# A retention layer's v made in its own head, with the next head's k and q projections between the head's steps

## The chip, the core and the metric

The kernel runs on one core of a Trainium2 chip. The metric is the device time of one launch in microseconds (us). The kernel before takes 1476.63 us, the median of three runs (1476.28 to 1478.8). The engines are named as the profile names them: PE is TensorE (matmuls; PEld are its weight loads), DVE is VectorE, ACT is ScalarE, POOL is GpSimd, SP is SyncE, which issues most of the DMAs.

## The reference

One inference step of a decoder with two layers, on 512 prompt tokens and 8 groups of 4 sample tokens together (544 columns). Layer 0 mixes with a short gated convolution, layer 1 with multi-scale retention; each is followed by a gated feed-forward part. The change lies in the retention layer (4 heads, keys of 256, values of 512, model width 1024):

```python
def retention_mixer(x, s0, pos, w_in, gn_g, w_out):
    q, k, v, g = jnp.split(x @ w_in, [1024, 2048, 4096], axis=-1)   # then by heads
    q, k = rotary(q, pos), rotary(k, pos) * 256 ** -0.5
    o, S = retention_chunkwise(q, k, v, s0)   # o = (q k^T * decay) v + q S0 * decay
    o = (o - mean(o)) * rsqrt(var(o) + 1e-6)                         # over a head's 512 values
    return (silu(g) * o * gn_g) @ w_out, S    # S: the new state, prompt and every sample row
```

## The kernel before

Activations stand with the model width on the partitions: 8 tiles of 128 x 544. Every f32 product is made of three rounded ones (hi x hi, hi x lo, lo x hi): `split` makes the rounded part on ACT (L188) and the rest on DVE (L189); `load_piece` brings a weight piece of 512 KB by SP and splits it, with three buffers for each of the raw piece, its high and its low part (tags `w`, `wh`, `wl`). `project` multiplies a piece with the activations: 8 k-tiles x 3 products x 2 halves of 272 columns, 48 matmuls on L175. PSUM has two double banks (`psum()`, printed as `mm`) and four single banks (`bank()`, printed as `sm`).

The order of the work is written by hand, and a planner that knows costs fixes the sequence on each engine: an instruction that is ready may go ahead of an earlier one that is not. `tc.issue_after(ins)` holds a block's instructions behind `ins` on their engine.

The stages are: convolution layer, feed-forward part 0, `ahead`, the four heads of retention, feed-forward part 1.

- `ahead` (L847 to 917) runs at the end of feed-forward part 0. It makes k and q of head 0, and completes R (L259), the broadcast of the token norms. In between stands `value_products(0, ...)`, which makes v of head 0 and sends it to DRAM (`v_made`). With R, `operand` makes on DVE and ACT the four operand tiles of the gate jobs, one for each pair of k-tiles, each of seven planes: planes 0 to 4 by a first split, 5 and 6 by a second. The tile that it works in has the tag `f` with two buffers. Then come six gate jobs (L461): gates of heads 0 to 2, each job a fast matrix product of seven products of 12 matmuls instead of eight (`Job`, `weights7`). Results go to DRAM (`gate_made`).
- A head `h` (L1299 to 1391) that has a next one starts with `value_products(h + 1, ...)`: 96 matmuls of 512 columns in four pieces (L816 to L818) and the sample tokens' share (L824). Through `first` and `then` this head's own v is loaded and split (`value_loaded`), the states are loaded (`states_load`), the head's q and k are split and transposed (`operands_made`), and the sample v is gathered (`value_sample`). `value_out` sends the next head's v to DRAM by ACT's queue. Then come `state` (the prompt's state, in two halves), `first_outputs` (the samples against their first state S0, its update, and the load of the fourth, S3, into its buffer), `scores`, `inner` 0 to 3, `normalized` (on DVE, with the root on POOL), `gated` (a transpose on PE, then a product with the gates on DVE), `states_update` (outer products, then two passes on DVE, L1258).
- Four `qk_project` for the next head stand among the later steps: k's two halves around the last states, with `states_update(h, st, 3)` inside the second, and q's two halves after the last `gated_pair`, right before `out_project`. A projection's end scales its half (`qk_rotate`, L1002), and after the second half `rotate` turns it (L1011 to 1016).
- `out_project` (L1261) splits the gated values (yh on ACT, yl on DVE) and multiplies them with four pieces of the output weights.
- Head 3 has no next head; its gates are made by four `gate_project` in the places of the others' projections.

Of the kernel before, what the change touches and what calls it, by code (L numbers as in the profile page):

```python
# [12 lines left out]
P = 128  # L13
# [35 lines left out]
def hybrid_decode_kernel(ctx: ExitStack, tc: tile.TileContext, a: dict, o: dict):  # L49
# [741 lines left out]
    v_made = [dram.tile([P, 5, DV], F32, tag=f"v{h}", name=nm("vm")) for h in range(NH)]  # L791
    gate_made = [dram.tile([P, 4, T], F32, tag=f"g{h}", name=nm("gm")) for h in range(AHEAD)]

    def value_piece(h, c, raw, adding=False, after=None, sw=None):
        return load_piece(a["rtv"][h, c], 2 * DV, keep=raw, adding=adding, after=after, sw=sw)

    def value_products(h, xs, first=None, then=None, ws=None, sw=None):

        pv = [bank() for _ in range(4)]
        pvs = psum()  # L800
        if ws is None:
            raw = []
            ws = [value_piece(h, c, raw, first is None, sw=None if c else sw) for c in range(2)]
        else:
            ws, raw = ws
        after = first() if first is not None else None
        for c in range(4):
            wh, wl = ws[c]
            if c < 2:
                ws.append(value_piece(h, c + 2, raw, first is None and c == 0, after=after if c == 0 else None))  # L810
            for k2 in range(2):
                kt = 2 * c + k2
                cw = slice(k2 * DV, (k2 + 1) * DV)
                for tt in range(4):
                    ts_, out = slice(tt * P, (tt + 1) * P), pv[tt]
                    nc.tensor.matmul(out, xh[kt][:, ts_], wh[:, cw], start=(kt == 0), stop=False)  # L816
                    nc.tensor.matmul(out, xh[kt][:, ts_], wl[:, cw], start=False, stop=False)  # L817
                    last = nc.tensor.matmul(out, xl[kt][:, ts_], wh[:, cw], start=False, stop=(kt == KT - 1))  # L818
            if c in (1, 2):

                with tc.issue_after(last.ins):
                    for g in range(4):
                        kt = 4 * (c - 1) + g
                        nc.tensor.matmul(  # L824
                            pvs[g * NS : (g + 1) * NS, 0, :], xs[:, kt, :],
                            raw[kt // 2][:, kt % 2 * DV : (kt % 2 + 1) * DV],
                            start=(c == 1), stop=(c == 2), skip_group_check=True,
                        )
            if then is not None:
                then(c)  # L830
        return pv, pvs

    def value_out(h, pv, pvs, places):

        for tt, (row, _) in enumerate(places):
            nc.scalar.activation(
                row, pv[tt] if tt < 4 else pvs[:, 0, :], AF.Copy, scale=rN[:, tt : tt + 1] if tt < 4 else rN[:, 5:6]
            )
            if places[tt][1] is not None:
                at, src = places[tt][1]  # L840
                nc.scalar.dma_start(v_made[h][:, at, :], src)
# [5 lines left out]
    def ahead(tp, fp, sw, one):  # L847
# [10 lines left out]
        qw, qpt = load_piece(a["rtqk"][0, 0], KT * P, adding=True), [bank(), bank()]  # L858
        project(qpt, *qw, 0, xh, xl, weave=steps)
# [11 lines left out]
        off(0, 0, qpt)  # L871
        xs = fp.tile([P, KT, NS], F32, tag="f", name=nm("xs"))
        sample_x(xs)

        def operand_of(c):
# [3 lines left out]
        va = [tp.tile([P, 2, T], F32, tag="gu", name=nm("va")) for _ in range(2)]  # L879
        vs = fp.tile([P, DV], F32, tag="f", name=nm("vs"))  # L880
        rows = [va[tt // 2][:, tt % 2, :DV] for tt in range(4)] + [vs]
        outs = [None, (slice(0, 2), va[0][:, :, :DV]), None, (slice(2, 4), va[1][:, :, :DV]), (4, vs)]
        qw = load_piece(a["rtqk"][0, 1], KT * P, adding=True)
# [38 lines left out]
    with ExitStack() as c2:  # L922
# [39 lines left out]
        def qk_start(h):  # L962

            st = {}
            gt = tp.tile([P, 2, T], F32, tag="gt", name=nm("gt"), bufs=1)
            nc.sync.dma_start(gt, a["gtab"][h])
            st["gt"] = gt
            st["rot"] = [
                tp.tile([P, 2, T], F32, tag=f"rot{w}", name=nm("rot"), bufs=1) for w in range(2)
            ]  # L970
            return st

        def qk_loaded(st):

            loads = [(st["rot"][1], qk_made[1]), (cos, a["rope"][0]), (sin, a["rope"][1]), (st["rot"][0], qk_made[0])]
            for t, src in loads:
                last = nc.sync.dma_start(t, src)
# [9 lines left out]
        def qk_project(h, st, which, dt, inside=None):  # L987

            wh, wl = load_piece(a["rtqk"][h, which * 2 + dt], KT * P)
            pt = [bank(), bank()] if dt else psum()  # L990
# [8 lines left out]
        def qk_rotate(st, which, dt, pt):  # L999
            r = st["rot"][which]  # L1000
# [24 lines left out]
        def value_loaded(h, st):  # L1025

            vw = tp.tile([P, 4, T], F32, tag="gate", name=nm("vw"), bufs=1)[:, :, :DV]
            vsw = tp.tile([P, DV], F32, tag="yn", name=nm("vsw"))
            nc.sync.dma_start(vw, v_made[h][:, 0:4, :])
            st["loaded"] = nc.sync.dma_start(vsw, v_made[h][:, 4, :])  # L1030
            vh = tp.tile([P, 4, DV], F32R, tag="vyh", name=nm("vh"), bufs=1)
            vl = tp.tile([P, 4, DV], F32R, tag="vyl", name=nm("vl"), bufs=1)
            for i in range(2):
                split(vh[:, 2 * i : 2 * i + 2, :], vl[:, 2 * i : 2 * i + 2, :], vw[:, 2 * i : 2 * i + 2, :])
            st["v"] = [vh, vl, vsw]
            if h < AHEAD:
                st["gate"] = tp.tile([P, 4, T], F32, tag="gate", name=nm("gate"), bufs=1)
                nc.sync.dma_start(st["gate"], gate_made[h])

        def value_sample(h, st):  # L1040

            pt = psum()
            v4 = tp.tile([P, 2, DV], F32R, tag="rot1", name=nm("v4"), bufs=1)
            split(v4[:, 0, :], v4[:, 1, :], st["v"][2])
            for i in range(2):
                nc.tensor.matmul(pt[:NS, 0, :], sum4, v4[:, i, :], start=(i == 0), stop=(i == 1))
            v2 = [tp.tile([NS, DV], F32R, tag=f"rt{i}", name=nm("v2"), bufs=1) for i in range(2)]
            split(*v2, pt[:NS, 0, :])
            st["v"][2] = v2
# [249 lines left out]
        for h in range(NH):  # L1299
            more = h + 1 < NH  # L1300
            st["S"] = {}

            def first():
                value_loaded(h, st)
                return st["loaded"] if h == 0 else None

            def then(c):
                if c == 0:
                    with tc.issue_after(last_load[0].ins) if h == 0 else ExitStack():
                        for i in range(2):  # L1310
                            states_load(h, st, i)
                elif c == 1:
                    states_load(h, st, 2)
                    operands_made(h, st)
                elif c == 2:
                    value_sample(h, st)

            if more:
                pv, pvs = value_products(h + 1, xs, first, then, None if h else next_v)
                va = tp.tile([P, 2, DV], F32, tag="rot1", name=nm("va"), bufs=1)  # L1320
                vb = [tp.tile([P, DV], F32, tag="yn", name=nm("vb")) for _ in range(2)]
                sample_operands(h, st)
                vc = tp.tile([P, DV], F32, tag="rt1", name=nm("vc"), bufs=1)
                rows = [va[:, 0, :], va[:, 1, :], *vb, vc]
                outs = [None, (slice(0, 2), va), (2, vb[0]), (3, vb[1]), (4, vc)]
                value_out(h + 1, pv, pvs, list(zip(rows, outs)))
                state(h, st, 0)
                first_outputs(h, st)
                state(h, st, 1)
            else:  # L1330
                gw = load_piece(a["rtg"][h, 0], KT * P)
                first()
# [181 lines left out]
```

## Time and profile before

| what | before |
| --- | --- |
| median of three runs | 1476.63 us |
| the profiled execution's own time | 1478.13 us |
| its span, first to last instruction | 1475.8 us |
| PE busy | 1458.5 us (99%) |
| DVE busy | 959.6 us (65%) |
| ACT busy | 610.5 us (41%) |
| POOL busy | 90.1 us (6%) |
| mean granted PE clock | 0.995 |
| DMA | 194.86 MB, mean 132 GB/s |

A busy time is the union of an engine's instructions in the one profiled execution; matmuls overlap in it, so the time from the start of one to the start of the next says more than the duration of one. The granted clock is the share of full speed at which PE was allowed to run. In the groups of instructions a row has: line, engine, operation, out<-in by tile names, shapes, count | busy us, mean ns of one | idle us of the engine just before them, and what ended it.

### The profile page before, as it was taken

Reading aid. Unit: us, or ns where it says so; the run is one execution under the profiler, and the core shown is the slowest. Engines: PE = TensorE matmul, PEld = TensorE weight load, DVE = VectorE, ACT = ScalarE, POOL = GpSimd, SP = SyncE. Lnnn points to the kernel's source line nnn. Section 1 sums busy time; section 2 is a strip of 40 time slices with the busy share of each in tenths; the row PEclk is TensorE's granted clock in tenths of the full one; section 3 lists DMA queues with packets and bytes.
Section 4 is the critical chain, followed back from the end, with each engine's and each line's share of the span. In section 5 each row is a group of like instructions: output and inputs, shape, how many; then the busy total and the mean of one; then the engine's idle time right before and its main releaser. Section 6 shows DMA issues by size and latency. Waiting matters only on the chain.

```text
span 1475.8 us, 26100 instructions
## 1 busy us (share of the span) xinstructions
PE 1458.5 (99%) x10944; PEld 1382.9 (94%) x10944; DVE 959.6 (65%) x1470; ACT 610.5 (41%) x882; POOL 90.1 (6%) x112
## 2 busy tenths in 40 slices
PE   9999999999999999999899999999999999999998
PEld 9999999999999999799589698798799999999997
DVE  6645439847748546776686484595759857748645
ACT  5222355625425335466412322323265625525424
POOL 0100220000000003000000000000030000000002
PEclk9999999999999999999999999999999999999999
DMA  6222274232222334554784573672454232322322
GB/s 225 86 87 86 89 177 109 96 105 87 93 93 100 98 90 132 140 169 149 274 287 140 197 257 115 210 248 102 157 146 112 94 107 86 99 93 96 101 65 83
DMA packets 77445, 194.86 MB, mean 132 GB/s; under 512 B 7168, under 2 KB 24448, under 8 KB 76944
## 3 DMA queue, kind: packets, MB, share of 16 engines
q1 hardware_dynamic: 70272, 172.83, 34.6%
q0 software_dynamic: 2912, 10.56, 4.1%
q10 hardware_dynamic: 4144, 9.81, 1.7%
q8 instruction: 86, 1.41, 0.4%
q14 instruction: 31, 0.25, 0.1%
HBM read 162.29 MB, written 30.88 MB: 131 GB/s over the span
## 4 chain that ended last, share of the span: by engine, by line
PE 94%; DVE 3%; DMA 1%; issue 1%; ACT 1%; POOL 0%; DVEq 0%; POOLq 0%; ACTq 0%; SPq 0%
PE mm L175 35%; PE sm L461 30%; PE sm L175 15%; PE sm L817 2%; PE sm L818 2%; PE sm L163 2%; PE sm L816 2%; PE sm L1237 1%; PE sm L164 1%; PE sm L165 1%; DVE wl L189 1%; DMA wl<-in_rtqk_dram 1%; PE mm L1253 0%; DVE xl L201 0%; PE mm L1192 0%
## 5 line engine op out<-in xcount | busy, mean ns | idle before, releaser
L188 ACT ACTIVATE wh<-w 128x1024 fp32r<-128x1024 f32 (+4 forms) x210 | 204.5, 977 | 382.8 <-PE mm L175 185.7
L189 DVE TENSOR_TENSOR wl<-w,wh 128x1024 fp32r<-128x1024 f32 (+4 forms) x210 | 236.9, 1131 | 42.5 <-ACT wh L188 40.4
L461 PE MATMUL sm<-oh,wh 128*128 128x272 f32 x672 | 194.5, 289 | 0.0
L461 PE MATMUL sm<-oh,wl 128*128 128x272 f32 x672 | 194.2, 289 | 0.0
L461 PE MATMUL sm<-ol,wh 128*128 128x272 f32 x672 | 194.0, 289 | 0.0
L175 PE MATMUL mm<-xh,wh 128*128 128x272 f32 x804 | 170.1, 292 | 0.2
L175 PE MATMUL mm<-xh,wl 128*128 128x272 f32 x804 | 167.0, 290 | 2.4 <-DMA wl<-in_rtqk_dram 2.4
L175 PE MATMUL mm<-xl,wh 128*128 128x272 f32 x804 | 166.8, 289 | 0.0
L269 DVE TENSOR_TENSOR x<-x,mm 128x544 f32<-128x544 f32 x85 | 61.3, 721 | 144.3 <-PE mm L175 144.1
L461 PE MATMUL sm<-oh,l 128*128 128x272 f32 x504 | 145.6, 289 | 0.0
L461 PE MATMUL sm<-ol,h 128*128 128x272 f32 x504 | 145.4, 289 | 0.0
L461 PE MATMUL sm<-oh,h 128*128 128x272 f32 x504 | 145.3, 289 | 0.0
L175 PEld LDWEIGHTS mm<-xh,wl 128*128 128x128 f32 x804 | 126.1, 190 | 3.2 <-DMA wl<-in_rtqk_dram 2.6
L175 PEld LDWEIGHTS mm<-xh,wh 128*128 128x128 f32 x804 | 126.7, 190 | 1.7 <-ACT wh L188 0.5
L461 PEld LDWEIGHTS sm<-oh,wh 128*128 128x128 f32 x672 | 126.8, 189 | 1.1 <-ACT u L518 0.6
L175 PEld LDWEIGHTS mm<-xl,wh 128*128 128x128 f32 x804 | 127.0, 190 | 0.1
L461 PEld LDWEIGHTS sm<-oh,wl 128*128 128x128 f32 x672 | 126.8, 189 | 0.0
L461 PEld LDWEIGHTS sm<-ol,wh 128*128 128x128 f32 x672 | 126.6, 188 | 0.0
L189 DVE TENSOR_TENSOR l<-w,h 128x1024 fp32r<-128x1024 f32 x84 | 80.3, 956 | 56.3 <-ACT h L188 56.0
L175 PE MATMUL sm<-xh,wh 128*128 128x272 f32 x476 | 101.6, 291 | 0.0
L175 PE MATMUL sm<-xh,wl 128*128 128x272 f32 x476 | 99.8, 288 | 0.0
L175 PE MATMUL sm<-xl,wh 128*128 128x272 f32 x476 | 99.5, 287 | 0.0
(290 smaller groups left out, 3049.4 us busy)
## 6 DMA issues: line engine op xcount, KB each, us to landing
w<-in_ffgu_dram SPq DMA_DIRECT2D x88, 512.0 KB, 3.5
w<-in_ffdn_dram SPq DMA_DIRECT2D x96, 192.0 KB, 2.5
S<-in_rets_dram SPq DMA_DIRECT2D x16, 1024.0 KB, 7.1
out_rets_dram<-S SPq DMA_DIRECT2D x16, 1024.0 KB, 4.6
w<-in_cvin_dram SPq DMA_DIRECT2D x21, 512.0 KB, 3.4
w<-in_rtv_dram SPq DMA_DIRECT2D x16, 512.0 KB, 3.7
w<-in_rtqk_dram SPq DMA_DIRECT2D x16, 512.0 KB, 4.3
w<-in_rtg_dram SPq DMA_DIRECT2D x16, 512.0 KB, 3.8
```

The lines of the kernel that those rows point to most:

```text
L163: nc.tensor.matmul(out, lh, rh, start=start, stop=False, skip_group_check=True)
L164: nc.tensor.matmul(out, lh, rl, start=False, stop=False, skip_group_check=True)
L165: last_product[0] = nc.tensor.matmul(out, ll, rh, start=False, stop=stop, skip_group_check=True)
L175: last_product[0] = nc.tensor.matmul(half(pt, hf)[:, :HT], w[:, c], act[k][:, hf * HT : (hf + 1) * HT], start=(first and k == ks[0] and i ...
L188: h = nc.scalar.activation(dh, src, AF.Copy)
L189: nc.vector.tensor_sub(dl, src, dh.bitcast(F32))
L269: last_residual[0] = nc.vector.tensor_add(xk, xk, p)
L461: nc.tensor.matmul(out, w[:, c], b[k][:, at, :], start=(first and k == 0 and i == 0), stop=(k == n - 1 and i == 2), skip_group_check=True,)
L816: nc.tensor.matmul(out, xh[kt][:, ts_], wh[:, cw], start=(kt == 0), stop=False)
L817: nc.tensor.matmul(out, xh[kt][:, ts_], wl[:, cw], start=False, stop=False)
L818: last = nc.tensor.matmul(out, xl[kt][:, ts_], wh[:, cw], start=False, stop=(kt == KT - 1))
L1237: last_product[0] = nc.tensor.matmul(st["po"][32 * g : 32 * g + 8, :], qm[:, dt, g, r, :], st["S"][i][:, g, :], start=False, stop=(i == 3) ...
```

## The change

v is made at the beginning of its own head, from PSUM straight into the two parts that the products read; nothing of v goes to DRAM. The four projections of the next head's k and q are spread: k's first half behind the values, k's second around `inner` 0, q's first around a `gated_pair` and `inner` 3, q's second around `states_update` 3 and the last `gated_pair`. In `ahead` head 0's q and k are made without v, copied by ACT without R (the scaling with R comes when they are read back), and the operands of the gate jobs are made while q's second half is projected. Head 3 makes its own v first, and its `first_outputs` stand behind the scores.

```diff
     def ahead(tp, fp, sw, one):
...
-        qw, qpt = load_piece(a["rtqk"][0, 0], KT * P, adding=True), [bank(), bank()]
-        project(qpt, *qw, 0, xh, xl, weave=steps)
+        qs = [load_piece(a["rtqk"][0, dt], KT * P, adding=True) for dt in range(2)]
+        qpts = [[bank(), bank()], psum()]
+        project(qpts[0], *qs[0], 0, xh, xl, weave=steps)
         drain(steps)
...
-            each(lambda p, d, r: nc.vector.tensor_mul(d, p, r), pt, halves(made[which][:, dt, :]), R)
+            each(lambda p, d: nc.scalar.activation(d, p, AF.Copy), pt, halves(made[which][:, dt, :]))
...
-        pv, pvs = value_products(0, xs, then=operand_of, sw=sw)
-        ...
-        value_out(0, pv, pvs, list(zip(rows, outs)))
-        qpt = psum()
-        project(qpt, *qw, 0, xh, xl)
-        off(0, 1, qpt)
+        for c in range(KP):
+            operand(c, fp, oh, ol, lambda kt: g_mix(1, kt))
+        project(qpts[1], *qs[1], 0, xh, xl)
+        off(0, 1, qpts[1])
...
-                next_v.extend(([value_piece(1, c, raw) for c in range(2)], raw))
+                next_v.extend(([value_piece(0, c, raw) for c in range(2)], raw))
...
             for which in (1, 0):
                 r = st["rot"][which]
+                qk_scale(st, which)
                 nc.vector.tensor_mul(r, r, st["gt"][:, which, :].unsqueeze(1).to_broadcast([P, 2, T]))
                 rotate(st, which)
...
+        def value(h, st, ws=None):
+            pv = [bank() for _ in range(4)]
+            pvs = psum()
+            ws, raw = ws or ([], [])
+            for c in range(4):
+                if len(ws) == c:
+                    ws.append(value_piece(h, c, raw))
+                ...          # 24 matmuls of a piece; after pieces 1 and 3 the sample tokens' share
+                if c == 1:
+                    operands_made(h, st)
+            ...              # sample v: v4 from pvs by ACT and DVE, gathered by sum4, split
+            for tt in range(4):
+                nc.scalar.activation(vh[:, tt, :], pv[tt], AF.Copy, scale=rN[:, tt : tt + 1])
+                nc.vector.scalar_tensor_tensor(
+                    vl[:, tt, :], pv[tt], rN[:, tt : tt + 1], vh[:, tt, :].bitcast(F32),
+                    op0=ALU.mult, op1=ALU.subtract,
+                )
+            st["v"] = (vh, vl, v2)
...
         for h in range(NH):
             more = h + 1 < NH
+            value(h, st, None if h else next_v)
             st["S"] = {}
+            for i in range(3):
+                states_load(h, st, i)
             if more:
+                st["gate"] = tp.tile([P, 4, T], F32, tag="gate", name=nm("gate"), bufs=1)
+                nc.sync.dma_start(st["gate"], gate_made[h])
+                nxt = qk_start(h + 1)
+                for which in (1, 0):
+                    qk_scale(nxt, which)
+                qk_project(h + 1, nxt, 1, 0)
+            else:
+                gate_project(h, st, 0)
+            sample_operands(h, st)
+            state(h, st, 0)
+            if more:
+                first_outputs(h, st)
+            else:
+                gate_project(h, st, 1)
+            state(h, st, 1)
+            for c in range(2):
+                scores(h, st, c)
+            if more:
+                yn = {}
+                def first():
+                    yn[0] = normalized(inner(h, st, 0))
+                    sample_outputs(h, st, 1)
+                    states_update(h, st, 1)
+                def second():
+                    gated_pair(h, st, (yn[0], 0), (yn[1], 1))
+                    yn[3] = inner(h, st, 3)
+                def third():
+                    states_update(h, st, 3)
+                    gated_pair(h, st, (yn[4], 4), (yn[3], 3))
+                qk_project(h + 1, nxt, 1, 1, first)
+                yn[1] = normalized(inner(h, st, 1))
+                sample_outputs(h, st, 2)
+                p2 = inner(h, st, 2)
+                qk_project(h + 1, nxt, 0, 0, second)
+                yn[2] = normalized(p2, "rt1")
+                with tc.issue_after(last_product[0].ins):
+                    sample_outputs(h, st, 3)
+                states_update(h, st, 2)
+                yn[3] = normalized(yn[3])
+                yn[4] = normalized(st["po"])
+                gated(h, st, yn[2], 2)
+                qk_project(h + 1, nxt, 0, 1, third)
                 out_project(h, st)
             else:
+                first_outputs(h, st)
+                ...          # inner 0 to 2 and the updates between them, as before
```

`qk_project` with a function as its last argument multiplies four k-tiles, calls the function, and multiplies the other four, into two single banks. The tile of the rotated q (`rot0`) is now taken when its first half is written, since `mid` of the head has the same buffer until `inner` 3.

More of the change, by code (lines that the diff above doesn't have):

```diff
@@ L790, in hybrid_decode_kernel @@
     qk_made = [dram.tile([P, 2, T], F32, tag=f"qk{w}", name=nm("qkm")) for w in range(2)]
-    v_made = [dram.tile([P, 5, DV], F32, tag=f"v{h}", name=nm("vm")) for h in range(NH)]
     gate_made = [dram.tile([P, 4, T], F32, tag=f"g{h}", name=nm("gm")) for h in range(AHEAD)]
[L794 to L841, printed above, removed]
+    def value_piece(h, c, raw):
+        return load_piece(a["rtv"][h, c], 2 * DV, keep=raw)
     def sample_x(xs):
@@ L967, in qk_start, with rotated @@
             st["gt"] = gt
[L968 to L971 removed]
+            st["rot"] = [None, rotated(1)]
+            return st
+        def rotated(which):
+            return tp.tile([P, 2, T], F32, tag=f"rot{which}", name=nm("rot"), bufs=1)
         def qk_loaded(st):
+            st["rot"][0] = rotated(0)
             loads = [(st["rot"][1], qk_made[1]), (cos, a["rope"][0]), (sin, a["rope"][1]), (st["rot"][0], qk_made[0])]
             for t, src in loads:
[L977 removed]
+                nc.sync.dma_start(t, src)
             for which in (1, 0):
                 r = st["rot"][which]
+                qk_scale(st, which)
                 nc.vector.tensor_mul(r, r, st["gt"][:, which, :].unsqueeze(1).to_broadcast([P, 2, T]))
@@ L989, in qk_project @@
             wh, wl = load_piece(a["rtqk"][h, which * 2 + dt], KT * P)
-            pt = [bank(), bank()] if dt else psum()
+            pt = [bank(), bank()] if inside else psum()
             if inside:
@@ L999, in qk_rotate @@
         def qk_rotate(st, which, dt, pt):
+            if which == 0 and dt == 0:
+                st["rot"][0] = rotated(0)
             r = st["rot"][which]
@@ L1040, in value_sample @@
[L1040 to L1049, printed above, removed]
+            for tt in range(4):
+                nc.scalar.activation(vh[:, tt, :], pv[tt], AF.Copy, scale=rN[:, tt : tt + 1])
+                nc.vector.scalar_tensor_tensor(
+                    vl[:, tt, :], pv[tt], rN[:, tt : tt + 1], vh[:, tt, :].bitcast(F32),
+                    op0=ALU.mult, op1=ALU.subtract,
+                )
@@ L1318, in hybrid_decode_kernel @@
-            if more:
[L1319 to L1332, printed above, removed]
-                for i in range(2):
-                    states_load(h, st, i)
-                gate_project(h, st, 0, lambda: operands_made(h, st), gw)
-                value_sample(h, st)
-                states_load(h, st, 2)
-                sample_operands(h, st)
-                state(h, st, 0)
-                first_outputs(h, st)
-                gate_project(h, st, 1)
-                state(h, st, 1)
@@ L1343, in hybrid_decode_kernel @@
-            for c in range(2):
-                scores(h, st, c)
-            yn0 = normalized(inner(h, st, 0))
-            sample_outputs(h, st, 1)
-            yn1 = normalized(inner(h, st, 1))
-            states_update(h, st, 1)
-            sample_outputs(h, st, 2)
-            p2 = inner(h, st, 2)
-            if more:
+            for i in range(3):
+                states_load(h, st, i)
+            if more:
+                st["gate"] = tp.tile([P, 4, T], F32, tag="gate", name=nm("gate"), bufs=1)
+                nc.sync.dma_start(st["gate"], gate_made[h])
```

78 lines of the change are left out of this document (30 added, 48 removed).

## The prediction

> **What bounds the kernel now.** I read the page's span and its chain first, then the waits of TensorE (PE) alone, then the window table around each wait, then the timelines of the three places that the diff rearranges.
>
> ```profile
> span 1475.8 us, 26100 instructions
> ...
> PE 94%; DVE 3%; DMA 1%; issue 1%; ACT 1%; POOL 0%; DVEq 0%; POOLq 0%; ACTq 0%; SPq 0%
> ```
>
> The chain that ends last is PE for 94%. The diff leaves the number and the shapes of the matmuls as they are: the value products of four heads, the 16 projections for q and k, the gates and the small sample products all stay, in another order. So the time can move only through the moments in which PE waits or runs at a lower clock. Before the change these are few (waits of PE: us in total, times, longest):
>
> ```profile
> PE mm L175 <- DMA wl<-in_rtqk_dram: 2.4, 1, 2.4
> PE sm L816 <- ACT wh L188: 2.3, 1, 2.3
> PE sm L817 <- DVE wl L189: 2.0, 1, 2.0
> ...
> PE sm L1192 <- DVE yn L1168: 0.6, 1, 0.6
> ```
>
> The first three lie in parts that the diff rewrites: one in `ahead`, before the gate jobs, two at the start of head 0. Heads 1 to 3 have no longer wait than the 0.6 of the last row, so a gain can come only from these places, and everything else can only be kept or lost. They also cost clock (the window table: busy us of PE, PEld, DVE, ACT and POOL, then the granted PE clock, DMA share and GB/s):
>
> ```profile
> 624.77:628.19 3.42, 3.42 (x18) 3.42 (x17) 1.05 (x2) 2.71 (x4) 0.00 (x0) 0.50 0.79 240
> 713.51:716.94 3.43, 3.43 (x8) 2.76 (x9) 3.43 (x8) 1.28 (x2) 0.00 (x0) 0.50 0.83 320
> ```
>
> Soon after the first wait, and after the last of the two at head 0, PE works for 3.4 us at half the clock, which loses 1.7 us each time.
>
> **Part 1: `ahead` without v.** Before, PE has q's first half, then head 0's value products, then q's second half, while R (the broadcast of the norm) is completed and VectorE (DVE) makes from it the operands of the gate jobs. The change takes the value products out of that place.
>
> ```profile
> 591.28 0.40 ACT L259 ACTIVATE R<-sm 128x272 f32<-128x272 f32 x1 [0.28 <-PE sm L227]
> 595.66 0.39 PE L816 MATMUL sm<-h,xh 128*128 128x512 f32 x1
> ```
>
> ```profile
> L189 DVE TENSOR_TENSOR ol<-f,oh 128x1360 fp32r<-128x1360 f32 (+1 forms) x8 | 9.2, 1150 | 6.1 <-ACT oh L188 6.1
> L534 DVE SCALAR_TENSOR_TENSOR f<-x,vec,R 128x544 f32<-128x544 f32 x8 | 6.0, 780 | 0.1
> L189 DVE TENSOR_TENSOR wl<-w,wh 128x1024 fp32r<-128x1024 f32 x2 | 2.4, 1218 | 0.0
> L404 DVE TENSOR_TENSOR f<-f 128x272 f32<-128x272 f32 x4 | 1.8, 441 | 0.1
> ...
> L403 DVE TENSOR_TENSOR f<-f 128x272 f32<-128x272 f32 x4 | 1.7, 435 | 0.0
> ```
>
> R is complete at 591.28 + 0.40 = 591.7. The four operands then cost DVE 9.2 + 6.0 + 7.0 = 22.2 us (the last are the four sums L403, L404, L406 and L407 of 1.7 to 1.8, of which the first and the last row are shown). The first product needs all four, but only their first split (planes 0 to 4), so the last operand's L406, L407 and second split, some 1.6 us, come after it: 20.6 us are left, and one of the weight splits of the first job (1.2 us) lies among them. With no bubble the last first split is done at 591.7 + 21.8 = 613.5. ACT's turn in the middle of each operand, which is the 6.1 us of idle time in the first row, hides now: `xs` no longer holds one of the two buffers of tag `f`, and the copies of k and q move from DVE to ACT. The rest of job 0's weight work fits before R, when DVE is idle:
>
> ```profile
> 580.00:592.00 12.00, 12.00 (x100) 12.00 (x100) 0.54 (x3) 5.05 (x7) 3.98 (x4) 1.00 0.58 117
> ```
>
> PE leaves q's first half at 595.66 and has one projection left. From the chain, a projection and a row of gate-job products:
>
> ```profile
> 630.83 60.68 PE sm L461 x480
> ```
>
> ```profile
> 748.60 5.97 PE mm L175 x48
> ```
>
> The projection ends at 601.6. A gate-job matmul takes 60.68/480 = 0.126 us. While the last operand is missing, products 1, 5 and 2 can run on three of their four k: 3 x 3 x 3 = 27 matmuls, 3.4 us. PE then idles 613.5 - 601.6 - 3.4 = 8.5 us if the planner interleaves them so, 11.9 if not, and perhaps 6 if weight splits stay out of DVE's way and products of the next job slip in. I take 8.5, and half of one half-clock stretch (0.9), since part of it would fall into the idle time. Gone are the 2.4 us wait and its 1.7. Sum: 8.5 + 0.9 - 4.1 = **+5.3** (ends +2 and +9.5).
>
> **Part 2: the start of head 0.** The place of the same instruction in three heads gives the cost of that start:
>
> ```profile
> 705.13 0.40 PE L817 MATMUL sm<-wl,xh 128*128 128x512 f32 x1
> 705.37 0.40 PE L818 MATMUL sm<-wh,xl 128*128 128x512 f32 x1
> 705.69 1.06 PE L824 MATMUL mm<-w,xs 128*32 128x512 f32 x8
> ```
>
> ```profile
> 815.23 1.07 PE L824 MATMUL mm<-w,xs 128*32 128x512 f32 x8
> ```
>
> ```profile
> 917.37 1.06 PE L824 MATMUL mm<-w,xs 128*32 128x512 f32 x8
> ```
>
> From head 0 to head 1 there are 109.5 us, from 1 to 2 102.1: head 0 loses 7.4. It waits because v comes back from memory:
>
> ```profile
> 705.06 2.01 ACT L188 ACTIVATE vh<-vw 128x1024 fp32r<-128x1024 f32 x2 [7.84 <-DMA vw<-vm]
> ```
>
> ```profile
> 706.15 1.22 DVE L189 TENSOR_TENSOR vl<-vw,vh 128x1024 fp32r<-128x1024 f32 x1 [2.26 <-ACT vh L188]
> ...
> 710.47 0.72 DVE L1016 TENSOR_TENSOR rot<-rot,rt 128x544 f32<-128x544 f32 x1
> ```
>
> ACT stands 7.8 us at this load with the weight split of piece 2 queued behind it, and DVE stands 2.3 us behind ACT with q's rotation queued behind v's split. After the change there is no such load. Pieces 0 and 1 are there as before; piece 2 has a free buffer and nothing that blocks SP in front of it. On DVE one split of 1.2 and a wait of 2.3 go, two scalings of `gt` (0.7 each, like any 128x544 product) and piece 2's split (1.2) come: q's rotation ends near 711.2 - 3.5 + 2.6 = 710.3. PE has piece 2's 24 matmuls, 0.24 apart, until 705.69 + 1.06 + 5.7 = 712.4, so it need not wait for the rotation. Piece 3 may come up to 2 us late, because its buffer is free only after L824. I take **-6.5** (ends -7.4 and -5).
>
> New on DVE are four evictions of v from PSUM; the nearest row is another PSUM read of this size:
>
> ```profile
> L1168 DVE TENSOR_SCALAR yn<-sm,mv,rs 128x512 f32<-128x512 f32 x5 | 4.0, 804 | 0.0
> ```
>
> Four of 0.8 come for two of 1.2 that go, under the k projection (6 us) that follows: 0, and 0.8 a head without that cover.
>
> **Part 3: the end of heads 0 to 2.** Here the change gives cover away.
>
> ```profile
> 874.97 0.60 PE L1192 MATMUL mm<-cb,yn 128*128 128x128 f32 x4
> ...
> 882.02 0.41 PE L175 MATMUL mm<-yh,wh 128*128 128x272 f32 x2
> 882.27 0.41 PE L175 MATMUL mm<-yl,wh 128*128 128x272 f32 x2
> ```
>
> ```profile
> 879.29 0.72 DVE L189 TENSOR_TENSOR yl<-gate,yh 128x544 fp32r<-128x544 f32 x1
> ```
>
> The last gated transposes end at 875.57 and `out_project` starts at 882.02: 6.45 us of projections cover the chain of gated product, yh on ACT, yl on DVE. The first yl is done at 880.01 and read at 882.27, so 2.3 us are spare. In the new order the last pair stands in the middle of q's second projection, with 3.0 us of cover: 1.2 us are uncovered by that alone. `states_update(h, st, 3)`, which stood inside k's second projection, now stands right before the pair:
>
> ```profile
> L1258 DVE SCALAR_TENSOR_TENSOR S<-S,mm 128x1024 f32<-128x1024 f32 x8 | 9.6, 1208 | 3.1 <-PE mm L1253 3.1
> ```
>
> Its two passes are ahead of the gated products on DVE: up to 2.4 more. q's own scaling and the rest of its rotation compete with yl as well. On the other side PE can begin the first k of three outputs before it needs the second yl (some 2 us). I take **3.0 a head, +9.0** for three (ends 0 and 6 a head). DVE is busy enough for this: 39 of 52 us in the stretch that ends there.
>
> ```profile
> 829.20:881.40 52.20, 52.20 (x348) 42.02 (x347) 39.18 (x64) 14.36 (x21) 3.56 (x5) 1.00 0.75 256
> ```
>
> **Part 4: the rest.** In the last head `first_outputs` moves behind the scores, so the fourth state, S3, gets its buffer later. Its update takes 2.4 us, and then comes the trip out and in:
>
> ```profile
> S<-in_rets_dram SPq DMA_DIRECT2D x16, 1024.0 KB, 7.1
> out_rets_dram<-S SPq DMA_DIRECT2D x16, 1024.0 KB, 4.6
> ```
>
> Together 14 us, against 18 inner products of 0.24 and one and a half gate projections of 6.0, 13 us, and some small products: +0.7 (0 to 3). In the other heads the loads of S0 to S2 now queue on SP behind the pieces of v, but v's own products and the k projection, over 20 us, stand before their use: 0, and up to one landing of 7.1 if that cover were gone. v's writes on ACT's queue and its loads on SP's are gone.
>
> Sum: 5.3 - 6.5 + 9.0 + 0.7 = **+8.5**. The profiled execution took 1478.13 (span 1475.8 and 2.3 around it), 1.5 above the median of 1476.63; so 1486.6 for its like, 1485.1 as a median.
>
> [...] The first wait above was 2.4 us, and the clock then fell to 0.50 for 3.42 us. [...]
>
> **Rivals.** *Cover holds at the tails* (11%, faster). It decides whether the first yl lands before q's last matmul; for it speaks that the planner interleaves the matmuls of several products, against it the 39 of 52 us. Then part 3 is 0, part 1 near its low end: 2.5 - 7 = -4.5, 1472. *Tails of about 1 us* (13%, no change): 4 - 6.5 + 3 = +0.5, 1477; that the planner restores the old order by itself, so that little changes, falls here. *Half clock at the tails too* (16%): tails of 5 and three times 1.7, 5.3 - 6.5 + 15 + 5 = +19, 1495.5. *The forecast* (60%): +3 to +15.
>
> **Numbers.** Two tenths of a per cent, about 3 us, is what a measurement of this kernel can tell from no change. The range leaves out most of the first rival and the far end of the third: 1476 to 1497. Faster 0.11, same 0.13, slower 0.76.
>
> **What would show it.** A PE wait on `oh` or `ol` of 6 us or more at the first gate job; no wait for the loads at head 0, and 102 to 104 us from its L824 to that of head 1; a wait at `out_project` for yl or yh in heads 0 to 2. I am wrong if these last are missing, if PE waits for weights or for S at a head's start, or if PE's busy time changes.

## The result, and the profile after

The changed kernel took 1501.5 us (median, 1499.7 to 1502.8) against 1477.7 for the kernel before beside it: a ratio of 1.016, interval 1.0147 to 1.0173. Forecast were 1485.1 and a range of 1476 to 1497. The direction was right; the loss was 23.8 us instead of 8.5, and above the range.

The profile page's span and the shares of the chain that ends last, after the change:

```profile
span 1499.5 us, 26034 instructions
...
PE 86%; DVE 8%; DMA 2%; issue 1%; ACT 1%; POOL 1%; SPq 0%; DVEq 0%; POOLq 0%; ACTq 0%
```

The span grew by 23.7 us. PE was 94% of that chain and is now 86%; VectorE was 3% and is now 8%, so it has come onto the path. What PE waits for (us in total, times, longest):

```profile
PE mm L175 <- ACT yh L188: 6.6, 4, 2.0
PE mm L1179 <- DVE rot L962: 5.0, 1, 5.0
PE sm L461 <- DVE ol L189: 3.5, 3, 1.6
PE mm L1160 <- DVE S L1226: 3.3, 3, 1.1
PE sm L461 <- ACT oh L188: 3.2, 1, 3.2
PE sm L461 <- DVE gate L521: 1.8, 2, 1.3
PE sm L461 <- ACT h L188: 1.5, 1, 1.5
```

The rows at L461 are the first gate jobs (part 1), the row on `rot` is the start of head 0 (part 2), and the rows on `yh` and `S` are the ends of the heads (part 3). Clock is lost as well. The window table of four stretches at half clock (busy us of PE, PEld, DVE, ACT and POOL, then the granted clock, DMA share, GB/s):

```profile
608.59:618.83 10.24, 8.25 (x33) 7.30 (x33) 9.97 (x15) 3.96 (x5) 0.00 (x0) 0.50 0.17 49
704.16:714.40 10.24, 7.38 (x21) 5.09 (x22) 8.35 (x16) 3.93 (x6) 0.00 (x0) 0.50 0.62 204
772.43:775.84 3.41, 3.41 (x18) 3.41 (x17) 3.41 (x6) 1.09 (x3) 0.00 (x0) 0.50 0.94 291
878.24:881.65 3.41, 3.41 (x16) 3.41 (x17) 3.41 (x6) 1.47 (x3) 0.00 (x0) 0.50 0.96 267
```

Estimated by the granted clock of 0.50, half of PE's busy time in each is lost: 4.1, 3.7, 1.7 and 1.7 us. The first sample product of each head (L824 before, L993 now), in PE's timeline, marks the heads:

```profile
691.29 0.64 PE L993 MATMUL mm<-w,xs 128*32 128x512 f32 x4
...
808.39 0.64 PE L993 MATMUL mm<-w,xs 128*32 128x512 f32 x4
...
915.11 0.64 PE L993 MATMUL mm<-w,xs 128*32 128x512 f32 x4
...
1020.29 0.64 PE L993 MATMUL mm<-w,xs 128*32 128x512 f32 x4
```

The three distances are 117.1, 106.7 and 105.2; before they were 109.5 for the first and 102.1 for the second. So a head now takes 3.1 us more with no half clock in it and 4.6 with one, and head 0 takes 10.4 more than the next head, where it took 7.4 more. That gives the account of the 23.7 us:

- Part 1: the waits at L461 add up to 10.0, the half clock to 4.1; before, 2.4 and 1.7 went there. **+10.0** (forecast +5.3).
- Part 2: 10.4 against 7.4. **+3.0** (forecast -6.5).
- Part 3: 4.6 + 4.6 + 3.1. **+12.3** (forecast +9.0).
- The rest, by subtraction: **-1.6** (forecast +0.7).

The start of head 0 in SyncE's timeline, and the row of its waits that stands for it:

```profile
680.40 0.94 SPq L1195 DMA_DIRECT2D S<-in_rets_dram  x2
681.42 0.45 SPq L908 DMA_DIRECT2D gt<-in_gtab_dram  x1
681.98 1.12 SPq L921 DMA_DIRECT2D rot<-qkm  x2
```

```profile
SPq L1195 <- PE sm L461: 12.7, 1, 12.7
```

Before, `gt`, k and q were issued long ahead of S, which was held behind the last weight load (SyncE's timeline of the kernel before):

```profile
677.89 0.38 SPq L966 DMA_DIRECT2D gt<-in_gtab_dram  x1
683.63 0.80 SPq L977 DMA_DIRECT2D rot<-qkm  x2
...
701.47 1.13 SPq L1227 DMA_DIRECT2D S<-in_rets_dram  x2
```

After, the loads of S stand ahead of `gt`, k and q. Their first buffers lie where the operands of the gate jobs lay, so SP stands for 12.7 us until the last gate jobs release them, and `gt`, k and q, which need not wait for that, are issued behind 2 MB of S. VectorE's timeline shows the consequence:

```profile
691.90 1.36 DVE L930 TENSOR_TENSOR gt<-gt,R 128x544 f32<-128x544 f32 x2 [8.15 <-DMA gt<-in_gtab_dram]
694.73 1.29 DVE L925 TENSOR_TENSOR rot<-rot,gt 128x1088 f32<-128x1088 f32 x1 [1.47 <-DMA rot<-qkm]
...
705.41 0.72 DVE L963 TENSOR_TENSOR rot<-rot,rt 128x544 f32<-128x544 f32 x1
```

q is rotated at 706.1, 14.8 us after the first sample product, and PE has run out of work by then.

### The profile page after: what moved, and what is told of

The parts are those of the page before. It is cut to its first block, busy times and chain, and to the rows that moved or that the text cites. A ratio compares the mean times of both kernels' runs of the same rounds, so it can differ in the third digit from the quotient of the medians.

```text
span 1499.5 us, 26034 instructions
## 1 busy us (share of the span) xinstructions
PE 1462.6 (98%) x10944; PEld 1388.7 (93%) x10944; DVE 963.2 (64%) x1472; ACT 600.9 (40%) x872; POOL 85.3 (6%) x109
## 4 chain that ended last, share of the span: by engine, by line
PE 86%; DVE 8%; DMA 2%; issue 1%; ACT 1%; POOL 1%; SPq 0%; DVEq 0%; POOLq 0%; ACTq 0%
PE mm L175 34%; PE sm L461 28%; PE sm L175 13%; PE sm L987 2%; PE sm L988 2%; PE sm L986 2%; DVE S L1226 2%; PE sm L163 1%; DMA w<-in_rtg_dram 1%; PE sm L164 1%; PE sm L165 1%; DMA rot<-qkm 1%; DVE wl L189 1%; DVE yn L1136 1%; POOL rs L223 1%
## 5 line engine op out<-in xcount | busy, mean ns | idle before, releaser
L189 DVE TENSOR_TENSOR wl<-w,wh 128x1024 fp32r<-128x1024 f32 (+4 forms) x213 | 240.5, 1133 | 47.3 <-ACT wh L188 45.2
L461 PE MATMUL sm<-oh,wh 128*128 128x272 f32 x672 | 195.6, 291 | 3.2 <-ACT oh L188 3.2
L461 PE MATMUL sm<-ol,wh 128*128 128x272 f32 x672 | 195.1, 290 | 3.5 <-DVE ol L189 3.5
L461 PE MATMUL sm<-oh,wl 128*128 128x272 f32 x672 | 195.0, 290 | 0.0
L175 PE MATMUL mm<-xh,wh 128*128 128x272 f32 x772 | 161.5, 290 | 0.0
L175 PE MATMUL mm<-xh,wl 128*128 128x272 f32 x772 | 159.8, 289 | 0.0
L175 PE MATMUL mm<-xl,wh 128*128 128x272 f32 x772 | 159.2, 288 | 0.0
L461 PE MATMUL sm<-oh,h 128*128 128x272 f32 x504 | 146.4, 290 | 3.3 <-DVE gate L521 1.8
L461 PE MATMUL sm<-oh,l 128*128 128x272 f32 x504 | 146.3, 290 | 0.0
L461 PE MATMUL sm<-ol,h 128*128 128x272 f32 x504 | 146.1, 290 | 0.0
L461 PEld LDWEIGHTS sm<-oh,wh 128*128 128x128 f32 x672 | 127.4, 190 | 4.8 <-ACT oh L188 3.7
L461 PEld LDWEIGHTS sm<-ol,wh 128*128 128x128 f32 x672 | 127.4, 190 | 4.4 <-DVE ol L189 4.4
L461 PEld LDWEIGHTS sm<-oh,wl 128*128 128x128 f32 x672 | 127.8, 190 | 0.0
L175 PEld LDWEIGHTS mm<-xh,wh 128*128 128x128 f32 x772 | 120.6, 188 | 3.9 <-DVE wl L189 2.5
L175 PEld LDWEIGHTS mm<-xl,wh 128*128 128x128 f32 x772 | 120.8, 188 | 0.3 <-DVE xl L201 0.2
L175 PEld LDWEIGHTS mm<-xh,wl 128*128 128x128 f32 x772 | 120.3, 188 | 0.6 <-DVE wl L189 0.2
L175 PE MATMUL sm<-xh,wh 128*128 128x272 f32 x508 | 112.3, 293 | 0.3 <-DVE rs L222 0.3
L175 PE MATMUL sm<-xl,wh 128*128 128x272 f32 x508 | 109.5, 288 | 0.0
L175 PE MATMUL sm<-xh,wl 128*128 128x272 f32 x508 | 109.1, 288 | 0.0
```

Source lines behind the costliest of these rows:

```text
L175: last_product[0] = nc.tensor.matmul(half(pt, hf)[:, :HT], w[:, c], act[k][:, hf * HT : (hf + 1) * HT], start=(first and k == ks[0] and i ...
L189: nc.vector.tensor_sub(dl, src, dh.bitcast(F32))
L461: nc.tensor.matmul(out, w[:, c], b[k][:, at, :], start=(first and k == 0 and i == 0), stop=(k == n - 1 and i == 2), skip_group_check=True,)
```

## The experiments

My theory: three separate losses (SyncE's queue at head 0, VectorE's order before the gate jobs, lost cover at the tails), each dearer by half-clock stretches. The rivals stand with each run. Differences are against 1501.5; the kernel before read 1478.1 to 1478.4 beside these runs and 1477.7 beside the changed one, so a difference across sessions is good to about 0.7. A mark in a trace is that of one execution, and the six of the changed kernel took 1499.66 to 1502.79, so a difference of about 1 us up to head 0 says nothing.

**State loads behind k and q (head 0).**

```
             for t, src in loads:
-                nc.sync.dma_start(t, src)
+                last_load[0] = nc.sync.dma_start(t, src)
+            st["loaded"] = last_load[0]
...
-            for i in range(3):
-                states_load(h, st, i)
+            with tc.issue_after(st["loaded"].ins) if h == 0 else ExitStack():
+                for i in range(3):
+                    states_load(h, st, i)
```

> After the change head 0 starts about 10 us late, where a gain of 6.5 was forecast. Theory A (queue of SyncE): the 1 MB loads of S wait 12.7 us on SP for the memory of the operand tiles, and gt and the two rot tiles stand behind them; with the S loads behind these, gt and rot land before the gate jobs end, the waits of 8.2, 1.5 and 5.0 us at the start of head 0 go: 1491 to 1493 us (-8 to -10), and 102 to 105 us from the first sample product of head 0 to that of head 1 less what k's projection takes out of place. Rival B (VectorE): two scalings of gt and q and k's rotations are what PE waits for, whatever the queue: 1499 or more (-2 at most). If S then comes late for its own use: 1495 to 1499.

Measured: 1494.96, -6.5. SyncE's timeline now has `gt`, k and q ahead of S, 12 us sooner; PE's timeline marks heads 0 and 1:

```profile
669.46 0.38 SPq L908 DMA_DIRECT2D gt<-in_gtab_dram  x1
669.94 0.86 SPq L921 DMA_DIRECT2D rot<-qkm  x2
681.67 0.39 SPq L1196 DMA_DIRECT2D S<-in_rets_dram  x1
```

```profile
692.56 0.64 PE L994 MATMUL mm<-w,xs 128*32 128x512 f32 x4
...
802.08 0.64 PE L994 MATMUL mm<-w,xs 128*32 128x512 f32 x4
```

The wait on `rot` is gone, the mean granted clock of the traced execution is 0.993 for 0.990, and the distance is 109.5 instead of 117.1: -7.6 in the head. The whole, -6.5, falls short of the -8 to -10 forecast: head 0 starts 1.3 later in this trace, and SyncE is that late already ahead of the edit (653.85 for 652.60 at the last gate weights). VectorE has the same scalings and rotations as before the edit, so rival B falls, and PE does not wait for a load of S. Against the 106.7 of the next head 2.8 are lost, where the kernel before lost 7.4: with this queue mended, part 2 is a gain of 4.6.

**Job 1's weights held behind the operands (ahead of the gate jobs).** In VectorE's timeline of the changed kernel, job 1's weight sums (L420 to L423) lie among the operands:

```profile
589.41 0.69 DVE L420 TENSOR_TENSOR w<-w 128x512 f32<-128x512 f32 x1
...
596.97 0.69 DVE L421 TENSOR_TENSOR w<-w,w 128x512 f32<-128x512 f32 x1 [2.44 <-DMA w<-in_rtg_dram]
...
612.30 2.21 DVE L189 TENSOR_TENSOR ol<-f,oh 128x1360 fp32r<-128x1360 f32 x2
```

There are four sums of 0.69 (two of them shown) and a wait of 2.44 for a load. The first sum ends before the operands begin at 590.61; the other three and the wait, 4.5 us, stand among them.

The hold, in which `last_operand` is the second split of the last operand:

```
...
             if nxt is not None:
-                nxt.prepare()
+                with tc.issue_after(last_operand[0].ins) if held and i == 0 else ExitStack():
+                    nxt.prepare()
```

> Job 1's weight sums and splits on VectorE, ScalarE and the loads' issue are held behind the last split of the operands of the gate jobs. Theory A (VectorE stands blocked behind job 1's sums, one of which waits 2.4 us for its load): the four operands come 4 to 6 us sooner, 1495 to 1498 us. Rival B: the operands are bound by R and their own 22 us, and job 1 then comes late for its own products: 1500 to 1504.

Measured: 1493.18, -8.3, more than either end. The operands' last splits of their first part, which ended at 612.30 + 2.21 = 614.5, now end at 609.5, five us sooner, in VectorE's timeline. PE's waits at the gate jobs fall from 10.0 to 4.7. The stretch of 10.24 at half clock, with 8.25 of work, is one of 6.83 with 6.02 (window table), which saves 1.1. Head 0 starts 7.3 us sooner (683.95); the last us of the 8.3 these rows do not explain.

```profile
606.46 3.06 DVE L189 TENSOR_TENSOR ol<-f,oh 128x1360 fp32r<-128x1360 f32 x2
```

```profile
607.27:614.10 6.83, 6.02 (x26) 6.02 (x27) 5.80 (x10) 2.13 (x4) 0.00 (x0) 0.50 0.01 2
```

**A dummy as cover.** q's second projection made twice, so that PE has 6 us more to do there.

```
-        project(qpts[1], *qs[1], 0, xh, xl)
+        for _ in range(2):
+            project(qpts[1], *qs[1], 0, xh, xl)
```

> The change, and q's second projection in front of the gate jobs made twice: 48 more matmuls, 6.0 us of PE, with the same result. Theory (what bounds the start of the gate jobs is VectorE's operands, PE having nothing to do; part 1 gives away cover): the added 6 us fill the idle time of the first gate products and the half-clock stretch behind it, so the time changes by -2 to +2: 1499 to 1503. Rival (PE and clock bound this place, or the operands only come by the same amount later): +6, 1507.

Measured: 1496.07. 48 matmuls more, and 5.4 us *less*. Neither had forecast a gain of that size. The four executions spread from 1494.29 to 1499.81 (mean granted clock 0.995 and 0.992), so the gain is 1.7 to 7.2 us; the one traced took 1494.56. PE's timeline:

```profile
688.20 0.64 PE L994 MATMUL mm<-w,xs 128*32 128x512 f32 x4
...
803.44 0.64 PE L994 MATMUL mm<-w,xs 128*32 128x512 f32 x4
...
908.61 0.64 PE L994 MATMUL mm<-w,xs 128*32 128x512 f32 x4
```

Up to head 0 it is 3.1 us ahead of the changed kernel: the 6.0 of work took the place of 9.1 us of idle time and half clock. The rest it gains later, 1.9 in head 0 and 1.6 in head 1, though the waits at the tails are the same to a tenth: head 1 takes the 105.2 that the changed kernel's head 2 takes with its tail at full clock (last section). With both edits, job 1's weights held and the dummy:

> Job 1's weights held, and q's second projection made twice (6.0 us more of PE, same result). If the four operands themselves still bound the start of the gate jobs once job 1's sums are out of the way (4.7 us of waits and a half-clock stretch of 6.8 us are left there, together some 8 us), the added work costs nothing: 1491 to 1495 against 1493.2. If the hold had already brought the operands early enough, so that little is left to cover: 1497 to 1499.

Measured: 1491.27, 1.9 below the hold alone. Up to head 0 the two traces are level (683.5 and 683.95), so even with the hold 6 us of work are hidden there: it is cover that the change gave away. At head 0 the wait on `rot` is 3.9 for 5.0, and the mean granted clock of the traced execution is 0.994 for 0.991.

**The tail covered.** Update 3 and the last gated pair ahead of q's whole second projection:

```
-                qk_project(h + 1, nxt, 0, 1, third)
+                third()
+                qk_project(h + 1, nxt, 0, 1, lambda: None)
```

> States update 3 and the last gated pair stand ahead of q's whole second projection (6 us of cover, as before the change), not in its middle. Theory A (cover): the waits on yh, yn and S at the ends of heads 0 to 2 (3.5 us each by the trace of after, and two half-clock stretches of 3.4 us) go: 1489 to 1494 us (-8 to -12). Rival B (VectorE is full at the tail, so the wait only moves to q's rotation or to the update itself): 1498.5 or more (-3 at most).

Measured: 1499.41, -2.1: my theory of cover fell, the rival held. The waits of PE on that kernel:

```profile
PE mm L175 <- ACT yh L188: 4.9, 4, 1.5
...
PE mm L1221 <- DVE S L1226: 1.4, 3, 0.5
```

Six us of cover instead of three take 0.5 from each wait on `yh`, but a head without half clock is only 0.1 us shorter (105.1 for 105.2). Most of the 2.1 is clock: in this trace the tail of head 1 is at full clock (1.00 from 873.13 to 879.95), and head 1 is 1.6 shorter. VectorE's timeline of head 2's tail shows why cover does so little (out_project starts on PE behind `yh`, which ScalarE makes of the product at 979.42):

```profile
969.36 0.81 DVE L1136 TENSOR_SCALAR yn<-sm,mv,rs 128x512 f32<-128x512 f32 x1 [0.72 <-POOL rs L223]
...
971.39 2.34 DVE L1226 SCALAR_TENSOR_TENSOR S<-S,mm 128x1024 f32<-128x1024 f32 x2
...
974.36 1.21 DVE L1226 SCALAR_TENSOR_TENSOR S<-S,mm 128x1024 f32<-128x1024 f32 x1
...
976.21 1.22 DVE L1226 SCALAR_TENSOR_TENSOR S<-S,mm 128x1024 f32<-128x1024 f32 x1
...
979.42 0.68 DVE L1163 TENSOR_TENSOR gate<-gate,mm 128x512 f32<-128x512 f32 x1
```

From the norm at 969.36, the last but one, to the last gated product VectorE has not a gap: four passes over S (two updates, 4.8 us), the last norm, a rotation's product and a weight split are the longest of what stands between them. With update 3 alone moved and the pair left in the middle:

> Only states update 3 stands ahead of q's second projection; the last gated pair stays in its middle. If the update's two passes of VectorE (2.4 us) are what makes the pair late: 1490 to 1495, nearly as much as with both moved. If the pair's place (3 us of cover instead of 6) is: 1497 to 1500. I expect 1495 to 1498: the 1.1 us wait on S goes and half of the wait on yh stays.

Measured: 1501.11, -0.4, above both ranges. VectorE has the order of the run above, and PE's waits are as good as there (5.0 on `yh`, 1.4 on S), so the pair's place gives nothing beyond the update's. But here the tail of head 2 has a stretch at half clock (0.50 from 983.28 to 986.69), and in the run above head 2 takes 105.0.

**VectorE relieved at the tail.** On top of the covered tail, state 3's product and update 2 go into the middle of q's first projection:

```
                     yn[3] = inner(h, st, 3)
+                    with tc.issue_after(last_product[0].ins):
+                        sample_outputs(h, st, 3)
+                    states_update(h, st, 2)
...
                 yn[2] = normalized(p2, "rt1")
-                with tc.issue_after(last_product[0].ins):
-                    sample_outputs(h, st, 3)
-                states_update(h, st, 2)
...
```

> As in the kernel with the tail covered (1499.4), and besides state 3's sample product and state update 2 stand in the middle of q's first projection, so that VectorE has two of the four passes over S (2.4 us) behind it when the last pair comes. Theory (VectorE, not PE's cover, is the limit of the tail: 14 us of its work in a row from the first norm to the last gated product): the 2.3 us that are left at each tail go, -5 to -7 against the covered tail: 1492 to 1495. Rival (the chain norm, transposes, gated product, split is as long as it is, whatever VectorE has besides): 1498 to 1500.

Measured: 1495.33, -4.1 against the covered tail and -6.2 in all; a little short of the theory, well past the rival. PE's timeline:

```profile
806.79 0.64 PE L993 MATMUL mm<-w,xs 128*32 128x512 f32 x4
...
910.75 0.64 PE L993 MATMUL mm<-w,xs 128*32 128x512 f32 x4
...
1014.69 0.64 PE L993 MATMUL mm<-w,xs 128*32 128x512 f32 x4
```

104.0 a head, against 105.1 with cover alone and 102.1 before. In each of the two traces heads 1 and 2 agree to 0.1 (104.0 and 103.9; 105.1 and 105.0), where 1.5 lie between a head with half clock and one without in the changed kernel, so the 1.1 a head is put down to the relief. In head 2 two passes over S instead of four stand between the last norm but one (970.63) and the last gated product (977.02), and 6.4 us instead of 10.1. The 1.8 that are left are now one wait on VectorE's reading of q's PSUM banks and one on `yl`:

```profile
PE sm L1160 <- DVE rot L949: 3.9, 3, 1.3
...
PE mm L175 <- DVE yl L189: 1.6, 3, 0.5
```

**All four together.**

> State loads behind k and q, job 1's weights held, tail covered, and VectorE relieved there, together. If the four losses are separate, they add up: -6.5, -8.3 and -7 to -9 (the covered tail and the relief): 1477 to 1480, about the time of the kernel before. If they share the half-clock stretches or VectorE's time: 1482 to 1488.

Measured: 1479.74, ratio to the kernel before 1.0011 (1.0002 to 1.002). The three gains, 6.5 + 8.3 + 6.2 = 21.0, add up: -21.8. So these places hold nearly the whole loss, and mended the new order is about as fast as the old one, 0.1% slower and not faster.

**The kernel before, mended.** Its own losses were 4.1 in `ahead` and 7.4 at head 0. q's second weight without the second load, and v's split at head 0 behind q's rotation:

```
-        qw = load_piece(a["rtqk"][0, 1], KT * P, adding=True)
+        qw = load_piece(a["rtqk"][0, 1], KT * P)
...
-            for i in range(2):
-                split(vh[...], vl[...], vw[...])
+            with tc.issue_after(rotated[0].ins) if h == 0 else ExitStack():
+                for i in range(2):
+                    split(vh[...], vl[...], vw[...])
```

> The kernel before, without this change, and its own two losses mended: q's second half for head 0 splits its weight on VectorE instead of waiting for a second load by GpSimd (2.4 us wait and a half-clock stretch, 4.1 in all), and the split of v at head 0 is held behind q's rotation (7.4 us over a steady head). Theory: 1466 to 1471. If VectorE's 1.2 us for the weight split delays the operands of the gate jobs by as much, and v's split then comes late for the first state product: 1474 to 1479.

Measured: 1473.78, ratio 0.997 (0.9959 to 0.9981): above the 1466 to 1471 of the theory, just under the other end's 1474. In `ahead` the wait of 2.4 us is gone, and the mean granted clock of the traced execution is 0.997 for 0.995, but the gate jobs wait 1.4 us for a weight split instead, and head 0 starts only 1.2 sooner (704.47 for 705.69). Head 0 itself is 2 us shorter. There PE waits 2.5 us for a value piece whose load was issued behind v. With that load first, then v, then the states (for h = 0):

```
-                value_loaded(h, st)
-                return st["loaded"] if h == 0 else None
+                if h:
+                    value_loaded(h, st)
...
+                    if h == 0:
+                        with tc.issue_after(st["rots"].ins):
+                            value_loaded(h, st)
...
```

> The mended kernel before (1473.8) and its loads at head 0 in another order on SyncE: the third value piece ahead of k, q and v, then v, then the states. In the mended one PE waits 2.5 us for the split of that piece, whose load was issued behind v's, and head 0 still takes 107.3 us against 102.15 of a steady one. If the load is the cause: 1469 to 1471. If v's split for the first state product or the rotations are what comes last: 1473 to 1476.

Measured: 1472.53, ratio 0.9964 (0.9951 to 0.9976), between the two ranges. PE's wait for that piece is gone; PE waits 1.4 us for the load of a value piece at L824 instead, and head 0 still takes 107.1, so what makes it long stays open. This is the fastest median, 0.36% under the kernel before, with an interval that overlaps that of the run above, and it keeps the old order.

## Why the prediction was wrong

**Part 2 is the step that failed**, by 9.5 of the 15 us between forecast and result. It said of piece 2 "nothing that blocks SP in front of it", and of the rotations that they would end before PE needed them. It followed the queue for the v pieces and left out the other loads of that place. The runs show in its place a wait of 12.7 us on SyncE's queue, `gt`, k and q behind it, a wait of 5.0 us of PE for q's rotation and a stretch of 10.24 us at half clock. The change moved the state loads out of the hold that had kept them behind the last load, and with that ahead of `gt`, k and q. The cost was named in part 4, "the loads of S0 to S2 now queue on SP behind the pieces of v", with 7.1 us if their cover were gone, and weighed only by when S itself is used, not by what stands behind S on the queue. The prediction's signs for this place failed with it: PE does wait for what the loads bring, and head 0 takes 117.1 us, not 102 to 104. With S held back, that head is 7.6 us shorter, and the start of head 0 is a gain of 4.6, a little under the forecast's low end of 5. One reading of the kernel before was short as well: the half clock at its head 0 lasts 6.83 us (710.11 to 716.94), not only the 3.43 that were read; with 0.7 us of work in its first half and 3.4 in its second it costs 2.1, by the clock of 0.50, and not 1.7, which the 7.4 measured for the head holds already.

**Part 1 was mis-sized**: +10.0 for +5.3. The bubble was there, on `oh` and `ol` as foretold, 6.7 us of waits there and 3.3 on later splits and sums of the gate jobs, 10.0 in all for 8.5. The clock was the larger miss: half a stretch (0.9) was taken, and it was a stretch three times as long with 8.25 us of work in it, 4.1. Job 1's weight sums, with a wait on a load among them, were not counted; the hold shows 5 us of delay in the operands and 7.3 up to head 0. That the last first split came at 614.5, near the 613.5 foretold, is luck: with job 1 held it takes 18.6 us from the first operand (590.91 to 609.52) where 21.8 were counted, and the two errors nearly cancel.

**Part 3 was about right**: 4.1 a head for 3.0, inside its range of 0 to 6, at the waits that were named (`yh`, and `S` before it). Without half clock it is 3.1; the other 1.0 is clock, which part 3 left to a rival. The reason given first, the pair's lost cover, was the lesser one: the covered tail made a head without half clock 0.1 shorter, and the relief of VectorE on top of it 1.1 more; the relief alone was not run. The second reason, VectorE's two passes over S ahead of the products, was the better one, and the passes were four. It too explains only part of the 3.1, since 1.8 stay.

**Part 4** came out at -1.6 for +0.7, by subtraction; no run tested it. The trace of the changed kernel shows no wait of PE for a load of S, in the last head or elsewhere.

Of the rivals, half clock at the tails came true in two of three heads, but with tails of 3.1 and not 5: waits of 2.04 us were followed by 3.41 us at a clock of 0.50 in heads 0 and 1.

## What to carry to other kernels

When a block of loads is moved, list what stands behind each of them on the issuing queue, and whether a load that must wait for memory, here for 12.7 us, now stands ahead of one that need not. Where one engine makes the operands of another, work that is given away as cover can be paid with idle time and with a lower clock after it: here with 10.0 us of waits at the gate jobs and 4.1 of clock, and 6 us of useless matmuls made the kernel 5.4 us faster in the median. Before a wait is put down to missing cover, look whether the engine waited for has a gap at all in the time before. And before a difference of 2 us is put down to an edit, count the stretches at half clock in both traces: here one of 3.41 us at 0.50 is worth 1.7.

## What the hardware showed

The four stretches at a clock of 0.50 in the changed kernel's table last 10.24, 10.24, 3.41 and 3.41 us. The two short ones, which start at 772.43 and 878.24, lie at the tails of heads 0 and 1; the tail of head 2 has none. In the window table, first the 3.41 us ahead of each of the two, then two windows of that length at the tail of head 2:

```profile
769.01:772.43 3.42, 1.39 (x11) 1.17 (x10) 3.40 (x6) 2.55 (x5) 0.00 (x0) 1.00 0.99 327
874.83:878.24 3.41, 1.38 (x12) 1.16 (x11) 3.39 (x7) 1.89 (x3) 0.00 (x0) 1.00 0.75 276
980.64:984.05 3.41, 2.18 (x18) 1.96 (x17) 3.41 (x6) 1.06 (x1) 0.00 (x0) 1.00 0.47 175
984.05:987.46 3.41, 2.60 (x20) 2.60 (x21) 3.39 (x8) 2.30 (x4) 0.00 (x0) 1.00 1.01 302
```

The three tails have the same wait of 2.04 us on `yh`. In heads 0 and 1 PE is idle for 2.0 us of the window shown, and the next 3.41 us are at 0.50; in head 2 PE is idle for 1.2 and 0.8 us of the two windows, and the clock reads 1.00 in both and in the 3.41 us behind them. So the 1.7 us of a tail do not go by the length of this wait alone. With the dummy, head 1 takes 105.2 for 106.7 with no instruction of it changed. Idle time in one window does not settle it either: with the dummy, 1.9 us in the first window at the tail of head 2 were followed by a clock of 1.00, and with all four edits 1.1 at the start of head 0 by one of 0.50 (window tables of the two kernels, the window and what follows it). What decides, no run here shows.

```profile
974.75:978.16 3.41, 1.54 (x13) 1.32 (x12) 3.41 (x7) 1.60 (x2) 0.00 (x0) 1.00 0.67 250
978.16:981.58 3.42, 3.25 (x25) 3.25 (x26) 3.39 (x7) 1.76 (x4) 0.00 (x0) 1.00 0.93 275
```

```profile
704.54:707.95 3.41, 2.29 (x14) 1.55 (x12) 3.38 (x6) 2.69 (x5) 0.00 (x0) 1.00 0.00 0
707.95:711.37 3.42, 3.42 (x18) 3.42 (x17) 3.42 (x5) 0.00 (x0) 0.00 (x0) 0.50 0.61 165
```
